# Gate tiles of a recurrence and a convolution moved beside attention heads, and kept in DRAM until they are used

## The chip, the cores and the metric

The kernel runs on one core of a Trainium2 chip. The metric is the device time of one execution in microseconds (us); lower is better. The core has a matrix engine (PE, with its weight loads as PEld), a vector engine (DVE), an activation engine (ACT), a general engine (POOL) and a queue for transfers (SP). Each takes its instructions strictly in its own order; engines wait for one another by semaphores.

## The reference

Two networks of two layers each run one after the other on 512 tokens of 1024 features in fp32. Only the second matters here. Each of its layers projects the normed input and mixes three branches, each with a gate:

```
h = rms_norm(x, norm_g[l]);  proj = h @ w_in[l]
y_nsa  = nsa_attention(...)            # 8 heads of 64: two softmax attentions and a compressed one
y_lru  = rg_lru(u_lru, ...)            # 4-tap conv, two block-diagonal gates, scan along time
y_conv = conformer_conv(ga, gb, ...)   # u = ga*sigmoid(gb); 31-tap conv; layer norm; silu; @ w_pw2
mixed  = concat(y_nsa * silu(z_nsa), y_lru * silu(z_lru), y_conv * silu(z_conv))
x = x + mixed @ w_out[l]
```

`z_nsa`, `z_lru` and `z_conv` are columns of `proj` (512 each), so they depend only on `h`.

## The kernel before

Each product is made of three matmuls of high and low halves (`mm3`, L213 to L215; "split" means that ACT writes the high half, L204 or L237, and DVE or POOL the rest, L206, L208, L238). `w_tiles` makes 128 output columns by 512 tokens at a time: 24 matmuls with 512 moving columns over K = 1024, called a dense tile here. Weights come in slabs of 512 KB through SP; for the gate columns the low halves were computed earlier and are loaded too (`stored`, L273).

The heads (`nsa`) work in halves of 256 tokens: scores (L382), softmax over DVE, ACT and POOL (L389 to L394), transposes (L417, L425), values (L432), the compressed part (L1357), and at the end of a half `av_out` (L439 on ACT, L440 on DVE). A half is a long chain of small matmuls with waits.

The order in which the program issues work is that of the Python code, which a scheduler at build time then merges: it interleaves the heads with whatever dense tiles are ready and stand near. `PLACES` says how many pieces of side work (`work`: four parts of the convolution with their 31 taps, L1412; `part(0)` and `part(2)` of the recurrence, which end in a square root, L1522, and scans, L1526; its two gates, L1530) are issued after each stage of `mix2`: here four after heads 0, 4, 1, 5, one after heads 2, 6, 3, 7, and the rest behind the second `gated`. Last comes `conv_out`: for each of four token blocks b0 to b3 a transpose (L1442), statistics (L1444, L1446), a reciprocal root in two small POOL instructions (L364, L365) and the normed block (L1448); then for each of four column tiles transposes (L1453), two activations (L1455, L1456), a product (L1457) and a split; then the four z_conv tiles (`z`, L1466), and at last the product with `w_pw2` (`pw`, 48 matmuls) and `w_out` (`out2`, 288 matmuls; its output adds to the residual y, which is loaded from DRAM into the four buffers of tag `ac`).

The words "H" and "the norm chain" below stand for the end of the last matmul of the last head (the last L1357) and for the way from there through `conv_out` to the first `pw` matmul.

Of the kernel before, what the change touches and what calls it, by code (L numbers as in the profile page):

```python
# [69 lines left out]
class Net:  # L70
# [15 lines left out]
    def name(self, s):  # L86
# [2 lines left out]

    BUFS = {  # L90
        1: dict(raw=4, xt=2, ph=2, ac=4, pt=4, s=9, tmp=2, tiny=10, tm=12, rs=4, os=2, wh=4, wl=4, qk=13, q4=3, q3=1, sig=3, m8=3, sc=3, lraw=2, llo=2),
        2: dict(raw=2, xt=2, ph=2, ac=4, pt=6, s=7, os=2, wh=4, wl=4, qk=12, q4=4, sig=3, zt=2, cg=4, nt=2, gt=2, cu=2, cv=3, lr=2, lw=2, tiny=10, tm=12, rs=4),
    }
    FIRST = {F32: dict(ac=(1024, 4), sc1=(256, 1), sc2=(384, 1), sc3=(512, 1), iw=(32, 1), lf=(24, 2)), F32R: dict(dv=(512, 1), row=(512, 1))}
    SECOND = {F32: dict(cu=(512, 2), cs=(512, 2), ct=(2048, 1), par=(192, 2), sp=(4, 2), gates=(96, 1), pos=(16, 2), tmp=(256, 2)), F32R: dict(vc=(512, 2), kc=(128, 1))}
# [8 lines left out]
    ORDER = 'ISFDftdxBbzy'  # L104
    VIA = "q"
    LOP2 = "01"
    PLACES = [0, 0, 0, 0, 0, 4, 1, 8]
    PBUFS = dict(mm=3, ss=2, tr=2, av=1, acc=1)

    def phase(self, block, kept):  # L110

        self.block = block
        self.hold = self.last_load.ins if block > 1 and self.last_load else None
        self.places = {}
        for dtype, tags in kept.items():
            at = self.kept[dtype]
            for tag, (words, n) in tags.items():
                self.places[tag] = [at + i * words for i in range(n)]
                at += n * words
            assert at <= self.KEPT[dtype]  # L120

    def t(self, tag, shape, dtype=F32):
        if tag in self.places:
# [1307 lines left out]

        return c, [lambda j=j: part(j) for j in range(4)]

    def conv_out(self, l, h, c, par):

        nc, a = self.nc, self.a
        norm = self.t("nt", [P, 4, T])
        for b in range(NT):
            tok = slice(b * P, (b + 1) * P)
            tr = self.ps("tr")  # L1440
            for j in range(4):
                nc.tensor.transpose(tr[:, j * P:(j + 1) * P], c[j][:, tok], self.ident)  # L1442
            st = self.small([P, 6])
            nc.vector.bn_stats(st, tr)  # L1444
            mv = self.small([P, 2])
            nc.vector.bn_aggr(mv, st)  # L1446
            r = self.rstd(mv[:, 1:2], 1e-6)
            nc.vector.tensor_scalar(norm[:, b], tr, mv[:, 0:1], r, op0=OP.subtract, op1=OP.mult)  # L1448
        act = []
        for j in range(4):  # L1450
            tr = self.ps("tr")
            for b in range(NT):
                nc.tensor.transpose(tr[:, b * P:(b + 1) * P], norm[:, b, j * P:(j + 1) * P], self.ident)  # L1453
            s, v = self.t("sig", [P, T]), self.t("cg", [P, T])
            nc.scalar.activation(v, tr, AF.Identity, scale=par["g"][:, j:j + 1], bias=par["b"][:, j:j + 1])  # L1455
            nc.scalar.activation(s, tr, AF.Tanh, scale=par["hg"][:, j:j + 1], bias=par["hb"][:, j:j + 1])  # L1456
            nc.vector.scalar_tensor_tensor(s, s, 1.0, v, op0=OP.add, op1=OP.mult)  # L1457
            t = self.t("qk", [P, 2, T], F32R)
            self.split(s, t[:, 0], t[:, 1], scale=0.5)
            act.append(t)  # L1460
        zs = self.t("nt", [P, 4, T])
        sz = [zs[:, j] for j in range(4)]

        def z(j, ps):
            s = sz[j]
            nc.scalar.activation(s, ps, AF.Tanh, scale=0.5)  # L1466
            nc.vector.scalar_tensor_tensor(s, s, 1.0, ps, op0=OP.add, op1=OP.mult)

        self.w_tiles(a["w_in"][l], [[(3864 + j * P, P)] for j in range(4)], h, z, lows=self.lows[l])
        out = []  # L1470

        def pw(j, ps):
            s = sz[j]
            nc.vector.tensor_mul(s, s, ps)
            out.append(self.mixed(s))

        self.hold = self.last_load.ins
        self.w_tiles(a["conv_w_pw2"][l], [[(j * P, P)] for j in range(4)], (_Stack(act, 0), _Stack(act, 1)), pw, K=4)
        return out

    def lru(self, l, h, par):

        nc, a = self.nc, self.a
        g, out = {}, {}
        blocks = self.t("pt", [P, 2, 4, P])
        nc.gpsimd.memset(blocks, 0.0)
        for i, name in enumerate(("lru_w_a", "lru_w_i")):
            src = a[name][l].rearrange("(j r) i o -> r i j o", r=2)
# [29 lines left out]
        def part(j0):  # L1518
            da, db = [self.t("lw", [P, 2, T]) for _ in range(2)]
            self.w_tiles(a["w_in"][l], [[(1816 + j * P, P)] for j in (j0, j0 + 1)], h,  # L1520
                         lambda j, ps: emit(j0 + j, ps, da[:, j], db[:, j]), lows=self.lows[l])
            nc.scalar.activation(db, db, AF.Sqrt)  # L1522
            for i in range(2):
                v = g[j0 + i]
                nc.vector.scalar_tensor_tensor(db[:, i], v, 0.5, db[:, i], op0=OP.mult, op1=OP.mult)
                nc.vector.tensor_tensor_scan(v, da[:, i], db[:, i], 0.0, OP.mult, OP.add)  # L1526

        def z(j, ps):
            s = self.gate_silu(ps)
            nc.gpsimd.tensor_mul(g[j], s, g[j])  # L1530
            out[j] = g[j]

        def gate(j0):
            self.w_tiles(a["w_in"][l], [[(2328 + j * P, P)] for j in (j0, j0 + 1)], h, lambda j, ps: z(j0 + j, ps),
                         lows=self.lows[l])

        return out, [lambda: part(0), lambda: part(2), lambda: gate(0), lambda: gate(2)]

    def mix2(self, l, h, tables):
        nc, a = self.nc, self.a  # L1540
        par = self.params2(l)
# [147 lines left out]
```

## Time and profile before

| | us |
|---|---|
| median of 3 runs (lowest, highest) | 2550.74 (2550.54, 2554.34) |
| the profiled execution's own time | 2551.98 |
| its span | 2550.2 |
| PE busy | 2472.7 (97%) |
| DVE, ACT, POOL busy | 1630.3, 1231.7, 729.7 |
| second network, layer 0: last head matmul, first `pw` matmul, last `w_out` matmul start | 2024, 2065.60, 2142 |
| layer 1: first `pw` matmul | 2465.78 |

PE's busy time counts each matmul from its start to its modelled end, and matmuls overlap; how closely they follow one another tells more. Where nothing waits, one with 512 columns starts every 0.23 us.

### The profile page before, as it was taken

To read this page: it belongs to the slowest core of one execution; us is meant where nothing else is said; L and a number is where in the kernel's file an instruction comes from. 1 tells how busy PE (TensorE), PEld (TensorE's weight loads), DVE (VectorE), ACT (ScalarE), POOL (GpSimd) and SP (SyncE) were. 2 spreads that over 40 slices of the span, in tenths; PEclk is the share of its full clock that TensorE was granted. 3 is DMA by queue.
4 is the path that set the end of the run, shared out by engine and by line. 5 is a ranking of instruction groups with operands and counts; after the bars stand their busy time and mean duration, and the time that the engine had idled before them with its cause. 6 is when DMAs were issued, how large, how long until landed. Compare 5 with 4: busy or idle time off the path is not lost.

```text
span 2550.2 us, 35074 instructions
## 1 busy us (share of the span) xinstructions
PE 2472.7 (97%) x12660; PEld 2097.7 (82%) x12660; DVE 1630.3 (64%) x3126; ACT 1231.7 (48%) x2271; POOL 729.7 (29%) x845
## 2 busy tenths in 40 slices
PE   8989999999999998999999999998999899999998
PEld 8878888888888887888888888887988688988777
DVE  4985865654344669659465544346699755589874
ACT  5665643344333255665323343233575742576760
POOL 5621560122110264206002122004353312353320
PEclk9999999999999999999999999999999999999999
DMA  5203225366543332132435656334444143554151
GB/s 167 83 16 85 74 83 187 123 197 224 170 161 94 96 85 66 46 86 82 133 119 169 203 190 222 93 97 121 140 143 130 43 150 114 149 153 127 51 178 40
DMA packets 276654, 312.00 MB, mean 122 GB/s; under 512 B 25792, under 2 KB 221696, under 8 KB 276480
## 3 DMA queue, kind: packets, MB, share of 16 engines
q1 hardware_dynamic: 276480, 309.76, 39.4%
q8 instruction: 100, 1.64, 0.3%
q14 instruction: 74, 0.61, 0.1%
HBM read 274.84 MB, written 34.87 MB: 121 GB/s over the span
## 4 chain that ended last, share of the span: by engine, by line
PE 82%; DVE 9%; ACT 3%; DMA 2%; issue 2%; POOL 1%; SPq 0%; DVEq 0%; ACTq 0%; POOLq 0%
PE mm L214 19%; PE mm L215 18%; PE mm L213 18%; PE ss L382 3%; PE av L432 3%; PE ss L214 3%; PE ss L215 3%; PE ss L213 3%; PE tr L417 2%; PE av L215 1%; PE av L214 1%; PE av L213 1%; PE tr L215 1%; PE tr L214 1%; PE tr L213 1%
## 5 line engine op out<-in xcount | busy, mean ns | idle before, releaser
L238 DVE TENSOR_TENSOR wl<-raw,wh 128x1024 fp32r<-128x1024 f32 (+3 forms) x308 | 392.8, 1279 | 326.9 <-ACT wh L237 317.9
L237 ACT ACTIVATE wh<-raw 128x1024 fp32r<-128x1024 f32 (+6 forms) x358 | 361.3, 1013 | 448.8 <-PE tr L215 176.9
L213 PE MATMUL mm<-xt,wh 128*128 128x512 f32 x1456 | 574.4, 394 | 2.1 <-DVE sig L1376 2.1
L215 PE MATMUL mm<-xt,wl 128*128 128x512 f32 x1456 | 572.2, 393 | 2.8 <-DVE wl L238 2.8
L214 PE MATMUL mm<-xt,wh 128*128 128x512 f32 x1456 | 573.8, 394 | 0.0
L215 PEld LDWEIGHTS mm<-xt,wl 128*128 128x128 f32 x1456 | 275.0, 189 | 59.0 <-DVE wl L238 4.4
L213 PEld LDWEIGHTS mm<-xt,wh 128*128 128x128 f32 x1456 | 275.1, 189 | 57.3 <-DVE sig L1376 2.5
L214 PEld LDWEIGHTS mm<-xt,wh 128*128 128x128 f32 x1456 | 274.9, 189 | 54.5 <-issue 0.5
L260 POOL TENSOR_TENSOR llo<-lraw,llo 128x1024 fp32r<-128x1024 f32 x48 | 116.3, 2435 | 378.3 <-ACT llo L259 363.4
L213 PE MATMUL mm<-wh,xt 128*128 128x256 f32 (+6 forms) x624 | 190.4, 311 | 10.1 <-ACT wh L237 8.8
L215 PE MATMUL mm<-wh,xt 128*128 128x256 f32 (+6 forms) x624 | 191.9, 310 | 5.8 <-DVE xt L206 5.7
L214 PE MATMUL mm<-wl,xt 128*128 128x256 f32 (+6 forms) x624 | 192.6, 311 | 2.4 <-DVE wl L238 1.6
L364 POOL TENSOR_SCALAR tiny<-tiny 128x1 f32<-128x1 f32 x24 | 11.9, 495 | 516.7 <-DVE tiny L863 477.7
L391 ACT ACTIVATE s<-s,tm 128x128 f32<-128x128 f32 (+1 forms) x216 | 120.5, 558 | 64.4 <-DVE tm L389 57.2
L214 PE MATMUL mm<-wl,qk 128*128 128x512 f32 x352 | 136.2, 390 | 0.0
L215 PE MATMUL mm<-wh,qk 128*128 128x512 f32 x352 | 136.0, 389 | 0.0
L213 PE MATMUL mm<-wh,qk 128*128 128x512 f32 x352 | 134.7, 389 | 0.0
L394 POOL TENSOR_SCALAR s<-s,tm,kept 128x128 f32<-128x128 f32 (+3 forms) x128 | 78.4, 612 | 195.0 <-DVE tm L393 174.0
L213 PEld LDWEIGHTS mm<-wh,xt 128*128 128x128 f32 x624 | 119.6, 194 | 12.8 <-ACT wh L237 9.2
L215 PEld LDWEIGHTS mm<-wh,xt 128*128 128x128 f32 x624 | 120.4, 193 | 8.3 <-DVE xt L206 7.2
L214 PEld LDWEIGHTS mm<-wl,xt 128*128 128x128 f32 x624 | 120.7, 194 | 5.4 <-DVE wl L238 2.5
L1412 DVE SCALAR_TENSOR_TENSOR acc<-kept,acc 128x511 f32<-128x511 f32 (+6 forms) x168 | 124.1, 739 | 1.6
(373 smaller groups left out, 5256.8 us busy)
## 6 DMA issues: line engine op xcount, KB each, us to landing
raw<-in_w_in SPq DMA_DIRECT2D x84, 512.0 KB, 4.2
raw<-in_w_ff_in SPq DMA_DIRECT2D x64, 512.0 KB, 4.0
raw<-in_w_ff_out SPq DMA_DIRECT2D x64, 512.0 KB, 3.8
raw<-in_w_in SPq DMA_DIRECT2D x104, 256.0 KB, 3.8
low<-llo SPq DMA_DIRECT2D x48, 512.0 KB, 2.8
wl<-low SPq DMA_DIRECT2D x48, 512.0 KB, 3.7
raw<-in_w_out SPq DMA_DIRECT2D x40, 512.0 KB, 3.8
lraw<-in_w_in SPq DMA_DIRECT2D x48, 256.0 KB, 6.1
```

Of the source, the lines that this page charges most:

```text
L213: mm(out, A[0], B[0], start=start, stop=False)
L214: mm(out, A[0], B[1], start=False, stop=False)
L215: mm(out, A[1], B[0], start=False, stop=stop)
L237: self.nc.scalar.activation(hi, raw, AF.Copy)
L238: (self.nc.gpsimd if self.lo_on_pool else self.nc.vector).tensor_sub(lo, raw, hi.bitcast(F32))
L260: nc.gpsimd.tensor_sub(lo, raw, lo.bitcast(F32))
L382: self.nc.tensor.matmul(s, u[:, tok], v[:, :n], start=i == 0, stop=i == len(k) - 1)
L391: nc.scalar.activation(p, p, AF.Exp, bias=m, scale=-1.0, accum_out=den)
L394: nc.gpsimd.tensor_scalar(p, p, r, 1.0 if gate is None else gate, op0=OP.mult, op1=OP.mult)
L417: nc.tensor.transpose(tr[:, kb * P:(kb + 1) * P], p[:, kb * P:(kb + 1) * P], self.ident)
L432: nc.tensor.matmul(av[:, 256 - m.shape[-1]:], v[:, kb], m, start=start and kb + i == 0, stop=stop and kb == n - 1 and i == 1)
L1412: nc.vector.scalar_tensor_tensor(acc[0][:, d:], u[:, :T - d], w[:, k], acc[0][:, d:], op0=OP.mult, op1=OP.add)
```

## The change

- `PLACES` becomes strings of piece names. After heads 0, 4, 1, 5: the four convolution parts and `part(0)` of the recurrence (`abcdp`). After heads 2, 6, 3, 7: the four z_conv tiles and the four z_lru tiles (`zgh`). Behind the second `gated`: `part(2)`, then `gated(0)` and `gated(2)` (`qmn`).
- A gate tile is finished as before (`gate_silu`) but goes to DRAM (`side_gates`: 8 writes of 256 KB a layer). It is read back later (`back`): z_conv as one read of 1 MB into `nt`, z_lru as two reads of 512 KB into the `lw` buffers, which hold `part(2)`'s coefficients before that. POOL then multiplies (L1546 of the changed kernel).
- The tag `ac` is gone; the residual's four buffers lie on the kept space of the convolution's input, side sums and result.

PE, DVE, ACT and POOL have as many instructions as before (12646, 3032, 2049, 850); SP has 22 more (774 to 796).

```diff
-        2: dict(raw=2, xt=2, ph=2, ac=4, pt=6, s=7, os=2, wh=4, wl=4, qk=12, q4=4, sig=3, zt=2, cg=4, nt=2, gt=2, cu=2, cv=3, lr=2, lw=2, tiny=10, tm=12, rs=4),
+        2: dict(raw=2, xt=2, ph=2, pt=6, s=7, os=2, wh=4, wl=4, qk=12, q4=4, sig=3, zt=2, cg=4, nt=2, gt=2, cu=2, cv=3, lr=2, lw=2, tiny=10, tm=12, rs=4),
-    PLACES = [0, 0, 0, 0, 0, 4, 1, 8]
+    PLACES = ["", "", "", "", "", "abcdp", "zgh", "qmn"]
+        if "cu" in self.places:
+            self.places["ac"] = [self.places["cu"][0] + i * 1024 for i in range(4)]
+    def side_gates(self, l, h, c0, js, dst):
+
+        def z(i, ps):
+            s = self.gate_silu(ps)
+            self.nc.sync.dma_start(dst[:, js[i]], s)
+
+        self.w_tiles(self.a["w_in"][l], [[(c0 + j * P, P)] for j in js], h, z, lows=self.lows[l])
+
+    def back(self, src, t):
+
+        with self.tc.issue_after(self.last_load.ins):
+            self.nc.sync.dma_start(t, src)
+        return t
+
...
-        zs = self.t("nt", [P, 4, T])
+        out = []
+        zs = self.back(zd, self.t("nt", [P, 4, T]))
         sz = [zs[:, j] for j in range(4)]
-
-        def z(j, ps):
-            s = sz[j]
-            nc.scalar.activation(s, ps, AF.Tanh, scale=0.5)
-            nc.vector.scalar_tensor_tensor(s, s, 1.0, ps, op0=OP.add, op1=OP.mult)
-
-        self.w_tiles(a["w_in"][l], [[(3864 + j * P, P)] for j in range(4)], h, z, lows=self.lows[l])
-        out = []
...
-        def z(j, ps):
-            s = self.gate_silu(ps)
-            nc.gpsimd.tensor_mul(g[j], s, g[j])
-            out[j] = g[j]
+        zd = self.dram([P, 4, T])
...
+        def gated(j0):
+            z = self.back(zd[:, j0:j0 + 2], self.t("lw", [P, 2, T]))
+            for i in range(2):
+                j = j0 + i
+                nc.gpsimd.tensor_mul(g[j], z[:, i], g[j])
+                out[j] = g[j]
...
+        zd = self.dram([P, 4, T])
+        work = dict(zip("pqghmn", lru), z=lambda: self.side_gates(l, h, 3864, (0, 1, 2, 3), zd))
+        work.update((k, lambda f=f: (f(), self.run(steps, len(steps)))) for k, f in zip("abcd", glu))
+
+        def more(place):
+            for k in self.PLACES[place]:
+                work[k]()
```

What this does to the order of the engines is seen at three places of layer 0 of the second network.

On PE, in the norm chain of the kernel before, the transposes of column tiles (L1453, tr from nt) stand among the matmuls of the z_conv tiles (mm from xt, the normed input):

```order
L215 MATMUL mm_18977<-xt_12749,wl_18947 128x512
L213 MATMUL mm_18977<-xt_12749,wh_18946 128x512
L214 MATMUL mm_18977<-xt_12750,wh_18946 128x512
L1453 MATMUL tr_18911<-kept_66,nt_18832 128x128 x4
L215 MATMUL mm_18977<-xt_12749,wl_18947 128x512
L213 MATMUL mm_18977<-xt_12749,wh_18946 128x512
L1453 MATMUL tr_18924<-kept_66,nt_18832 128x128 x4
L214 MATMUL mm_18977<-xt_12750,wh_18946 128x512
L215 MATMUL mm_18977<-xt_12749,wl_18947 128x512
L213 MATMUL mm_18977<-xt_12749,wh_18946 128x512
```

In the changed kernel, at the same place (L1458 and L1469 are its transposes, mm from qk is `pw`), only matmuls of `w_out` (av, ss from wh and wl) are left ahead, and none between:

```order
L217 MATMUL av_19186<-wh_19222,qk_18967 128x512
L217 MATMUL ss_19187<-wh_19222,qk_18967 128x512
L217 MATMUL ss_19188<-wh_19222,qk_18967 128x512
L1458 MATMUL tr_19022<-kept_66 128x128 x4
L1469 MATMUL tr_19035<-kept_66,nt_18982 128x128 x4
L1469 MATMUL tr_19048<-kept_66,nt_18982 128x128 x4
L1469 MATMUL tr_19061<-kept_66,nt_18982 128x128 x4
L1469 MATMUL tr_19074<-kept_66,nt_18982 128x128 x4
L215 MATMUL mm_19095<-qk_19045,wh_19091 128x512
L215 MATMUL mm_19112<-qk_19045,wh_19091 128x512
L215 MATMUL mm_19135<-qk_19045,wh_19131 128x512
L216 MATMUL mm_19095<-qk_19045,wh_19091 128x512
```

The dense tiles have gone ahead of the last heads: of the 144 dense matmuls of gate tiles that lay between H and `pw`, none is left there; 18 of `w_out` are.

On POOL, at the end of a layer's heads, before: the roots of b0 to b3 (tiny) and the multiplies of the recurrence's gates (gt):

```order
L364 TENSOR_SCALAR tiny_18842<-tiny_18840 128x1
L365 TENSOR_TENSOR tiny_18842<-tiny_18842,kept_66 128x1
L364 TENSOR_SCALAR tiny_18855<-tiny_18853 128x1
L365 TENSOR_TENSOR tiny_18855<-tiny_18855,kept_66 128x1
L364 TENSOR_SCALAR tiny_18868<-tiny_18866 128x1
L365 TENSOR_TENSOR tiny_18868<-tiny_18868,kept_66 128x1
L1530 TENSOR_TENSOR gt_18436<-sig_18705,gt_18436 128x512
L1530 TENSOR_TENSOR gt_18436<-sig_18734,gt_18436 128x512
L364 TENSOR_SCALAR tiny_18881<-tiny_18879 128x1
L365 TENSOR_TENSOR tiny_18881<-tiny_18881,kept_66 128x1
L1530 TENSOR_TENSOR gt_18613<-sig_18775,gt_18613 128x512
L1530 TENSOR_TENSOR gt_18613<-sig_18804,gt_18613 128x512
```

The same in the changed kernel (L366 and L367 the root, L1546 the multiplies, lw the tile read back, "x2" two in a row):

```order
L366 TENSOR_SCALAR tiny_18992<-tiny_18990 128x1
L367 TENSOR_TENSOR tiny_18992<-tiny_18992,kept_66 128x1
L366 TENSOR_SCALAR tiny_19005<-tiny_19003 128x1
L367 TENSOR_TENSOR tiny_19005<-tiny_19005,kept_66 128x1
L366 TENSOR_SCALAR tiny_19018<-tiny_19016 128x1
L367 TENSOR_TENSOR tiny_19018<-tiny_19018,kept_66 128x1
L1546 TENSOR_TENSOR gt_17710<-lw_18950,gt_17710 128x512 x2
L1546 TENSOR_TENSOR gt_18895<-lw_18954,gt_18895 128x512 x2
L366 TENSOR_SCALAR tiny_19031<-tiny_19029 128x1
L367 TENSOR_TENSOR tiny_19031<-tiny_19031,kept_66 128x1
```

All four multiplies now stand ahead of the root of b3.

On DVE, changed kernel, the same place (L1462 statistics, L1464 the normed block, L210 splits; qk from gt is the recurrence's output):

```order
L1464 TENSOR_SCALAR nt_18982<-tr_18996,tiny_19003,tiny_19005 128x512
L1462 BN_AGGR tiny_19016<-tiny_19014 128x2
L1464 TENSOR_SCALAR nt_18982<-tr_19009,tiny_19016,tiny_19018 128x512
L1460 BN_STATS tiny_19027<-tr_19022 128x6
L1462 BN_AGGR tiny_19029<-tiny_19027 128x2
L210 SCALAR_TENSOR_TENSOR qk_18970<-gt_17710,qk_18970 128x512
L210 SCALAR_TENSOR_TENSOR qk_18973<-gt_17710,qk_18973 128x512
L210 SCALAR_TENSOR_TENSOR qk_18976<-gt_18895,qk_18976 128x512
L210 SCALAR_TENSOR_TENSOR qk_18979<-gt_18895,qk_18979 128x512
L1464 TENSOR_SCALAR nt_18982<-tr_19022,tiny_19029,tiny_19031 128x512
L1473 SCALAR_TENSOR_TENSOR sig_19040<-sig_19040,cg_19041 128x512
```

The four splits of the recurrence's output, which wait for POOL's multiplies, stand ahead of the normed block b3. Before, one of the four stood ahead of it and three behind.

## Rows read from the trace of the kernel before

**Rows 1.** The page: the chain that ended last, by engine.

```profile
PE 82%; DVE 9%; ACT 3%; DMA 2%; issue 2%; POOL 1%; SPq 0%; DVEq 0%; ACTq 0%; POOLq 0%
```

**Rows 2.** Layer 0: length, busy us (instructions) PE, PEld, DVE, ACT, POOL; clock, DMA.

```profile
1914.00:1960.00 46.00, 46.00 (x255) 39.71 (x254) 42.80 (x101) 27.59 (x62) 15.11 (x21) 1.00 0.45 129
1960.00:2010.00 50.00, 44.73 (x274) 36.45 (x272) 40.91 (x132) 32.27 (x89) 17.31 (x29) 0.99 0.12 40
2010.00:2040.00 30.00, 28.17 (x128) 20.56 (x128) 25.59 (x45) 26.71 (x43) 7.85 (x11) 0.96 0.27 89
2066.00:2142.40 76.40, 76.40 (x341) 63.19 (x341) 32.50 (x45) 16.65 (x19) 4.46 (x7) 1.00 0.35 107
```

**Rows 3.** Dense matmuls of 1914 to 1960, then 1960 to 2010, L215's third.

```profile
L215 PE MATMUL mm<-xt,wl 128*128 128x512 f32 x47 | 18.5, 394 | 0.0
...
L215 PE MATMUL mm<-xt,wl 128*128 128x512 f32 x11 | 4.3, 391 | 0.0
```

**Rows 4.** Layer 1's stretches that answer to layer 0's second and third.

```profile
2360.00:2410.00 50.00, 44.64 (x274) 35.81 (x274) 40.78 (x132) 34.05 (x94) 17.77 (x30) 1.00 0.11 36
2410.00:2440.00 30.00, 27.35 (x119) 20.00 (x119) 25.79 (x43) 26.20 (x41) 7.61 (x11) 0.94 0.24 73
```

**Rows 5.** PE's timeline around two gaps: start, length, instruction, idle time before.

```profile
2036.35 0.50 PE L213 MATMUL mm<-xt,wh 128*128 128x512 f32 x1 [1.83 <-DVE sig L1376]
2036.69 0.40 PE L214 MATMUL mm<-xt,wh 128*128 128x512 f32 x1
...
2434.74 0.33 PE L1453 MATMUL tr<-kept,nt 128*128 128x128 f32 x1 [1.87 <-DVE nt L1448]
...
2435.72 0.63 PE L214 MATMUL mm<-xt,wh 128*128 128x512 f32 x1
...
2438.28 0.63 PE L214 MATMUL mm<-xt,wh 128*128 128x512 f32 x1
```

**Rows 6.** DVE's half ends among the heads alone, 1970 to 2010.

```profile
L440 DVE TENSOR_TENSOR os<-av,kept 64x256 f32<-64x256 f32 x6 | 2.5, 416 | 0.4 <-ACT kept L439 0.2
```

**Rows 7.** Timeline: last head matmul, half end, normed b3, first pw matmul.

```profile
2023.78 0.45 PE L1357 MATMUL av<-qk,kept 128*128 128x256 f32 x2
...
2027.47 0.42 DVE L440 TENSOR_TENSOR os<-av,kept 64x256 f32<-64x256 f32 x1
...
2041.63 0.80 DVE L1448 TENSOR_SCALAR nt<-tr,tiny,tiny 128x512 f32<-128x512 f32 x1
...
2065.60 0.39 PE L213 MATMUL mm<-qk,wh 128*128 128x512 f32 x1
```

**Rows 8.** Instructions of the norm chain, 2010 to 2066, by line and form.

```profile
L1530 POOL TENSOR_TENSOR gt<-sig,gt 128x512 f32<-128x512 f32 x4 | 6.3, 1577 | 5.0 <-DVE gt L1526 4.7 <-DVE sig L1376 0.3
L1526 DVE TENSOR_TENSOR_SCAN gt<-lw,lw 128x512 f32<-128x512 f32 x4 | 4.7, 1210 | 0.0
L1456 ACT ACTIVATE sig<-tr,kept 128x512 f32<-128x512 f32 x4 | 3.2, 795 | 0.0
L208 DVE SCALAR_TENSOR_TENSOR qk<-gt,qk 128x512 fp32r<-128x512 f32 x4 | 3.1, 786 | 1.2 <-ACT qk L204 1.2
L1444 DVE BATCH_NORM_STATS2 tiny<-tr 128x6 f32<-128x512 f32 x4 | 2.8, 695 | 0.4 <-PE tr L1442 0.4
L365 POOL TENSOR_TENSOR tiny<-tiny,kept 128x1 f32<-128x1 f32 x4 | 2.6, 647 | 0.3
L1448 DVE TENSOR_SCALAR nt<-tr,tiny,tiny 128x512 f32<-128x512 f32 x4 | 3.2, 803 | 1.2 <-POOL tiny L365 1.2
L204 ACT ACTIVATE qk<-gt 128x512 fp32r<-128x512 f32 x4 | 2.5, 632 | 2.0 <-POOL gt L1530 1.9
L364 POOL TENSOR_SCALAR tiny<-tiny 128x1 f32<-128x1 f32 x4 | 1.7, 425 | 19.9 <-DVE tiny L1446 19.8
L1375 ACT ACT_TABLE_LOAD x1 | 1.3, 1283 | 0.0
```

**Rows 9.** DMA issues, 1900 to 2150: KB each, median us to landing.

```profile
wl<-low SPq DMA_DIRECT2D x12, 512.0 KB, 3.6
```

More of the change, by code (lines that the diff above doesn't have):

```diff
@@ L1432, in conv_glu, with conv_out @@
         return c, [lambda j=j: part(j) for j in range(4)]
-    def conv_out(self, l, h, c, par):
+    def side_gates(self, l, h, c0, js, dst):
[7 more added lines that the diff above has]
+        return t
+    def conv_out(self, l, c, par, zd):
         nc, a = self.nc, self.a
@@ L1526, in part @@
                 nc.vector.tensor_tensor_scan(v, da[:, i], db[:, i], 0.0, OP.mult, OP.add)
-        def z(j, ps):
-            s = self.gate_silu(ps)
-            nc.gpsimd.tensor_mul(g[j], s, g[j])
-            out[j] = g[j]
+        zd = self.dram([P, 4, T])
         def gate(j0):
-            self.w_tiles(a["w_in"][l], [[(2328 + j * P, P)] for j in (j0, j0 + 1)], h, lambda j, ps: z(j0 + j, ps),
-                         lows=self.lows[l])
-        return out, [lambda: part(0), lambda: part(2), lambda: gate(0), lambda: gate(2)]
+            self.side_gates(l, h, 2328, (j0, j0 + 1), zd)
+        def gated(j0):
[4 more added lines that the diff above has]
+                out[j] = g[j]
+        return out, [lambda: part(0), lambda: part(2), lambda: gate(0), lambda: gate(2), lambda: gated(0), lambda: gated(2)]
     def mix2(self, l, h, tables):
@@ L1544, in mix2 @@
         y, lru = self.lru(l, h, par)
-        work = [lambda f=f: (f(), self.run(steps, len(steps))) for f in glu] + lru
-        more = lambda place: self.run(work, self.PLACES[place])
+        zd = self.dram([P, 4, T])
[4 more added lines that the diff above has]
+                work[k]()
         proj = self.nsa_project(l, h, tables, more)
@@ L1572, in mix2 @@
         first = [self.mixed(x[j]) for x in (nsa, y) for j in range(4)]
-        return first + self.conv_out(l, h, c, par)
+        return first + self.conv_out(l, c, par, zd)
     def mixed(self, s):
```

## The prediction

> **What bounds the kernel now.** The chain that ended last is PE for 82% of the span [rows 1], so a change is worth what it does to the time in which PE waits or runs its matmuls further apart than it could. PE's busy share does not show that: its matmuls overlap, and a stretch can read as nearly full while they start late. So I read the stretches around the change [rows 2], and in each I count the matmuls and price them by the pace at which they follow one another where nothing waits. A dense one takes 0.2275 us (341 matmuls, 336 of them dense, fill 76.4 us, [rows 2]). In 1914 to 1960, where dense tiles and heads are mixed, 255 records stand in 46 us, 140 of them dense (47 for each of two lines, 46 for the third, [rows 3]); these take 31.9 us, which leaves 14.1 us for 115 small ones, 0.12 us each. That is just their pace when they run back to back (0.11 for 128 columns, 0.12 for 256, 0.18 for 384), so **a mixed stretch loses nothing**. In 1960 to 2010 there are 274 records with only 32 dense (11, 11, 10, [rows 3]): 7.3 us, and 242 small ones at 0.126 make 30.5, so 37.8 of 50 us are work and **12.2 us are lost**. This is where the heads run alone, from 1970 on. From 2010 to 2040 the same count gives 3.3 us lost: one gap of 1.83 us before a z tile [rows 5] and a granted clock of 0.96 over 30 us (1.2 us) [rows 2]. After 2040 nothing is lost. Layer 0 thus loses about 16 us. Layer 1, counted the same way, loses 12.5 us in 2360 to 2410 and 5.5 in 2410 to 2440, together 18, with a clock of 0.94 and a gap of 1.87 [rows 4, 5].
>
> The change removes no matmul and adds none. What it is worth is the losses after, less these 16 and 18.
>
> **The heads.** The z_conv and z_lru tiles and `part(0)` go beside the heads. By the order of the changed kernel the dense tiles last until about two and a half halves before the end; only 78 head matmuls or so stand without them. Alone, the heads lost 11.9 us over 40 us with 6 half ends [rows 2, 6], 2 us a half. So 2.5 halves lose 5 us. Where they are mixed the loss is zero now; but DVE was busy for 42.8 of 46 us there [rows 2], 93%. `part(0)` brings 11.9 us of DVE work (two tiles with four taps, two products, a scan each) beside 10.9 us of its own dense matmuls, which makes 54.7 of 56.9 us, 96%. Still below PE, but the heads wait for DVE at many places: I add 1 us (bounds 0 and 5, the latter if all that DVE gets in addition beyond its present share comes late). Sum for the heads **6 us**, bounds 2 (one half alone, DVE hidden) and 12 (no better than now).
>
> When does this end? The orders differ first at about 1913 us. From there to H the changed order holds 356 dense matmuls (81.0 us), 24 and 22 score matmuls of 512 and 384 columns (9.4), 154 of 256 (18.2), 196 of 128 (22.0) and eight block-diagonal ones of the recurrence (6.9): 137 us. With 6 lost, H is at about 2056, against 2024 before [rows 7]; 32 us later, because 144 dense matmuls have gone ahead of it.
>
> **The norm chain.** Before, those 144 dense matmuls, 32.8 us, lay between H and `pw` and covered the chain from the last head to the activated tiles; `pw` started 41.4 us after H [rows 7]. After, PE has between H and `pw` 28 transposes and 18 `w_out` matmuls, 7.2 us. So the chain becomes visible. I walk it from H, with durations of [rows 8] unless said otherwise.
> 1. The last half end on DVE came 3.7 us after the last head matmul before [rows 7]; the same instructions surround it after. PE's next `w_out` matmuls reuse its bank, so they start at H+3.7, and the transposes of b2 behind them end at 6.4.
> 2. DVE then has a scan (1.2), statistics of b1 (0.7), b0 normed (0.8), the gate product (0.7), b1's mean (0.2), statistics of b2 (0.7), the split of the last nsa tile (0.7), b1 normed (0.8): 9.5 and b2's mean 9.7. POOL's root of b2 (0.43 and 0.65) ends at 10.8.
> 3. POOL has the four multiplies next, 1.577 each: 17.1. They wait for nothing else, as far as I see: the read-backs use the buffers of `part(2)`, free after its last scan at about H+5, and 512 KB land 3.6 us after issue [rows 9].
> 4. Behind the multiplies stands b3's root (1.1: 18.2), and on DVE the four splits of the recurrence's output (0.63 on ACT and 0.79 after the last multiply: 18.5) and then b3 normed: 19.4.
> 5. Transposes (0.3), the first activation (0.8), an activation table (1.3), the second (0.8), the next tile's two, which stand ahead of the first split (1.3), the split (0.6): `pw` starts at **H+24.5**.
>
> Of these PE works 7.2 and waits **17.3 us**. Bounds: with multiplies as short as a scan (1.2) and the half end 2 us earlier, 14; from above, the kernel before had b3 normed 18.2 us after H [rows 7] with two multiplies ahead of its root where there are now four, which gives 21.4 in place of 19.4, and a read-back that takes twice the 3.6 us [rows 9], behind the 1 MB of z_conv, adds 1: 20.
>
> **The clock.** After its gap of 1.87 us layer 1's matmuls started 0.43 us apart (seven in 2.56 us, of which the first and the last stand in [rows 5]), at a granted clock of a half, 1.2 GHz, in place of 0.23; after the gap of 1.83 in layer 0 they went on at the full 2.4 GHz [rows 5]. With the one ahead of them that is eight dense matmuls at 0.2 us more each, 1.6. A wait of some 10 us on end is longer than both; I take **1.6 us** a layer, bounds 0 and 3.2. The Trainium skill (TensorE: Matmul & The Clock Gate, "Loop structure matters more than you think") says that a matmul after a long wait runs cold, and that products should follow one another without such waits; it speaks against this change. One of the two gaps of this trace agrees with it, the other does not; by the page alone the term is certain, by the rows it may be absent, and the forecast would be 3 us lower.
>
> **Others.** The residual's last four loads now wait for the transposes of the convolution's result (H+10) and are wanted when the first `w_out` tile is finished, after `pw`: later than H+28. Even at three times the 3.6 us of a load of 512 KB [rows 9] they are covered; without that cover they would cost PE those 11 us. The write-backs of 256 KB and two more waits on SP lie among weight loads of the mixed stretch, of which PE waited for none. Behind the reads on SP stand those residual loads and the `w_out` slabs after the first four; the slabs are wanted after `pw`, too. From `pw` on, 302 dense matmuls are left, as fast as now.
>
> **Sum.** Layer 0: 6 + 17.3 + 1.6 = 24.9 lost after, 16 before: +8.9. Layer 1: 24.9 against 18: +6.9. Together **+15.8 us**: 2567.8 for the profiled execution's 2551.98, or on the median, 1.2 below it, **2566.5**.
>
> **Rivals.**
> - *No change* (2546 to 2556). Heads filled better and the chain short: 2 + 14 + 1 = 17 a layer, as now. For it: the mixed stretch loses nothing today. Against it: PE must wait behind POOL's 6.3 us in every case.
> - *Faster*, about 2541. It takes losses below 13 a layer, 3 to 5 under those of today. The mechanism is the last halves: if the dense tiles reach to the end of the heads (loss 0) and the statistics of the blocks run while the last half is still under way, so that the roots of b0 to b2 are past when the half ends, the multiplies start at H+6 and `pw` at H+19.5: 12 lost. It decides from a `pw` start of some H+19. Against it: the transposes of b2 and b3 stand behind `w_out` matmuls that wait for the half end.
> - *DVE the bound* of the mixed stretch: the heads lose 12 as before, 31 a layer, +28: 2579. For it: 96%.
> - *The read-back late*: landing at H+16 in place of 9, behind 1 MB and the residual, moves the multiplies by 5: +26, 2576. Against it: the transfers have room (a DMA share of 0.12 in 1960 to 2010, [rows 2]).
>
> **How the numbers follow.** The forecast has a chance of 0.55 (2556 to 2575), no change 0.15, faster 0.11, DVE 0.13, read-back 0.06. Within 0.2% (5.1 us, about what a measurement here can tell from no change) thus lies 0.15, below it 0.11, above 0.74. The range leaves a tenth at either end: 2547 to 2582.
>
> **What would show it.** Right: H near 2056 and `pw` near 2081 in layer 0, PE with waits of 15 to 20 us between, ended by DVE's normed b3 and ACT's activations; POOL's four multiplies in one piece ahead of b3's root; PE's loss in 1970 to 2010 near zero. Wrong: `pw` within 20 us of H, or H past 2062, or PE waiting for transfers.

## The result, and the profile after

| | before | after |
|---|---|---|
| median in one comparison, us (runs) | 2552.4 (4) | 2567.32 (4) |
| lowest, highest | 2550.54, 2554.34 | 2565.39, 2569.01 |
| ratio of the times, 95% interval | | 1.0055, 1.0043 to 1.0067 |
| profiled execution, its span | 2551.98, 2550.2 | 2565.39, 2563.6 |

The changed kernel is 14.9 us (0.55%) slower. The forecast was 2566.5, 15.8 above the 2550.74 of the kernel before that it started from.

The page of the changed kernel gives the chain that ended last, by engine, and the answer to [rows 1]:

```profile
PE 82%; DVE 9%; ACT 3%; issue 2%; DMA 2%; POOL 1%; SPq 0%; DVEq 0%; POOLq 0%; ACTq 0%
```

PE's share is what it was; on this level nothing can be seen. The stretches show more. These are the windows of the changed kernel, with the columns of [rows 2]; the last line is layer 1's norm chain:

```profile
1914.00:1960.00 46.00, 46.00 (x251) 38.88 (x249) 44.07 (x99) 27.82 (x61) 18.62 (x22) 1.00 0.41 137
1960.00:2010.00 50.00, 49.37 (x262) 41.36 (x261) 34.50 (x89) 33.75 (x69) 9.47 (x15) 1.00 0.59 188
2010.00:2040.00 30.00, 29.53 (x175) 25.59 (x174) 19.15 (x57) 19.03 (x44) 11.81 (x13) 1.00 0.19 58
2040.00:2060.00 20.00, 17.23 (x96) 12.72 (x96) 16.59 (x38) 17.04 (x33) 3.86 (x6) 1.00 0.20 58
2060.00:2090.00 30.00, 18.04 (x67) 14.10 (x68) 20.50 (x31) 13.82 (x20) 9.89 (x12) 0.72 0.31 105
2090.00:2152.00 62.00, 62.00 (x277) 51.39 (x276) 29.86 (x43) 13.90 (x16) 3.48 (x6) 1.00 0.34 115
...
2463.00:2493.00 30.00, 17.86 (x67) 14.11 (x68) 20.55 (x30) 13.86 (x20) 9.89 (x12) 0.72 0.32 111
```

Before, PE's poor stretch was 1960 to 2010, where the heads ran alone [rows 2]. Now that stretch is full (49.37 of 50 us, and transfers of 188 GB/s in place of 40), and the poor one is 2060 to 2090: PE is busy for 18.04 of 30 us, at a granted clock of 0.72. It lies behind the heads, and layer 1 has its like.

Now the norm chain, in the timeline of the changed kernel (PE, DVE, POOL, ACT and SP's queue, put together in order of time; answers to [rows 7]):

```profile
2058.26 0.46 PE L1359 MATMUL av<-qk,kept 128*128 128x256 f32 x2
2061.48 0.42 DVE L442 TENSOR_TENSOR os<-av,kept 64x256 f32<-64x256 f32 x1
2061.96 0.51 PE L215 MATMUL av<-wh,qk 128*128 128x512 f32 x1 [2.80 <-DVE os L442]
2062.31 0.89 SPq L1447 DMA_DIRECT2D lw<-spill  x2
2062.69 0.63 PE L217 MATMUL av<-wh,qk 128*128 128x512 f32 x1
...
2065.25 0.62 PE L217 MATMUL av<-wh,qk 128*128 128x512 f32 x1
...
2068.88 0.55 POOL L367 TENSOR_TENSOR tiny<-tiny,kept 128x1 f32<-128x1 f32 x1
2069.39 5.82 POOL L1546 TENSOR_TENSOR gt<-lw,gt 128x512 f32<-128x512 f32 x4
2070.33 0.33 PE L1469 MATMUL tr<-kept,nt 128*128 128x128 f32 x1 [1.01 <-DVE nt L1464]
2071.35 5.28 DVE L210 SCALAR_TENSOR_TENSOR qk<-gt,qk 128x512 fp32r<-128x512 f32 x4 [0.26 <-ACT qk L206]
2075.90 0.55 POOL L367 TENSOR_TENSOR tiny<-tiny,kept 128x1 f32<-128x1 f32 x1
2076.55 0.80 DVE L1464 TENSOR_SCALAR nt<-tr,tiny,tiny 128x512 f32<-128x512 f32 x1
2077.41 3.04 PE L1469 MATMUL tr<-kept,nt 128*128 128x128 f32 x13 [6.75 <-DVE nt L1464]
2078.70 1.28 ACT L1472 ACT_TABLE_LOAD   x1
2082.68 1.65 PE L215 MATMUL mm<-qk,wh 128*128 128x512 f32 x3 [2.24 <-ACT qk L206]
2084.13 0.63 PE L216 MATMUL mm<-qk,wh 128*128 128x512 f32 x1
2084.56 0.63 PE L217 MATMUL mm<-qk,wl 128*128 128x512 f32 x1
```

H is 2058.72 (2058.26 and 0.46). PE then waits four times: 2.80 for the last half end, 1.01 and 6.75 for normed blocks, 2.24 for the first activated tile, 12.8 us together. POOL's four multiplies start 1.3 us ahead of the longest wait and run on through it in one piece; b3's root follows them, and on DVE the four splits stand in the same stretch. `pw` starts at 2082.68, H+24.0. Twice the dense matmuls run 0.43 us apart: from 2062.69 to 2065.25 six steps take 2.56, and from 2084.13 to 2084.56 one takes 0.43. The 13 transposes from 2077.41 on follow one another at 0.21 (3.04 us for all), about twice the 0.11 that the prediction prices for one of 128 columns.

The DMA issues of the changed kernel from 1900 to 2150 (KB each, median us to landing), for the transfers that are new:

```profile
nt<-spill SPq DMA_DIRECT2D x1, 1024.0 KB, 4.8
lw<-spill SPq DMA_DIRECT2D x2, 512.0 KB, 4.6
```

Counted and priced as in the prediction, from the first to the last head matmul ("heads") and from H to 5 us past the start of `pw` ("end"), PE loses this, layer 0 / layer 1 in us:

| | heads | end | of it waits | and half clock | `pw` after H | layer's length |
|---|---|---|---|---|---|---|
| before | 14.0 / 13.1 | 2.0 / 4.8 | 1.8 / 2.6 | 0 / 1.6 | 41.4 / 44.1 | 262.8 / 264.2 |
| after | 6.0 / 6.1 | 18.5 / 18.1 | 12.8 / 12.7 | 2.9 / 2.6 | 24.0 / 23.8 | 271.3 / 270.5 |

(The length is that from the first matmul of the heads' compressed part to the last of `w_out`; "half clock" is the number of matmuls that stand 0.43 apart by 0.2 us, so it leaves the slow transposes out.) The losses grow by 8.5 and 6.3, and the layers by 8.5 and 6.3: inside these stretches the account is closed. Outside them the two executions differ too. The changed kernel comes to layer 0 2.2 us later, and its way from the last `w_out` matmul of layer 0 to the first of the heads' compressed part in layer 1 takes 131.9 us in place of 135.5, at a granted clock of 0.99 in place of 0.96. So the spans differ by 13.4 us, not by 14.8.

### The profile page after: what moved, and what is told of

It reads as the page before. It is cut to its first block, busy times and chain, and to the rows that moved or that the text cites. A ratio compares the mean times of both kernels' runs of the same rounds, so it can differ in the third digit from the quotient of the medians.

```text
span 2563.6 us, 35115 instructions
## 1 busy us (share of the span) xinstructions
PE 2468.6 (96%) x12660; PEld 2098.8 (82%) x12660; DVE 1631.8 (64%) x3126; ACT 1233.7 (48%) x2271; POOL 734.0 (29%) x845
## 4 chain that ended last, share of the span: by engine, by line
PE 82%; DVE 9%; ACT 3%; issue 2%; DMA 2%; POOL 1%; SPq 0%; DVEq 0%; POOLq 0%; ACTq 0%
PE mm L216 19%; PE mm L215 19%; PE mm L217 19%; PE ss L384 3%; PE ss L217 3%; PE ss L216 3%; PE ss L215 3%; PE av L434 3%; PE tr L419 2%; PE av L215 1%; PE av L216 1%; PE av L217 1%; PE tr L217 1%; PE tr L216 1%; PE tr L215 1%
## 5 line engine op out<-in xcount | busy, mean ns | idle before, releaser
L240 DVE TENSOR_TENSOR wl<-raw,wh 128x1024 fp32r<-128x1024 f32 (+3 forms) x308 | 393.2, 1280 | 303.3 <-ACT wh L239 288.2
L215 PE MATMUL mm<-xt,wh 128*128 128x512 f32 x1456 | 573.0, 394 | 0.2
L215 PEld LDWEIGHTS mm<-xt,wh 128*128 128x128 f32 x1456 | 274.6, 189 | 54.2 <-DVE sig L1378 0.6
L215 PE MATMUL mm<-wh,xt 128*128 128x256 f32 (+6 forms) x624 | 189.9, 311 | 10.1 <-ACT wh L239 8.9
L366 POOL TENSOR_SCALAR tiny<-tiny 128x1 f32<-128x1 f32 x24 | 12.6, 526 | 505.2 <-DVE tiny L865 476.5
L215 PE MATMUL mm<-wh,qk 128*128 128x512 f32 x352 | 134.8, 389 | 0.0
L215 PEld LDWEIGHTS mm<-wh,xt 128*128 128x128 f32 x624 | 119.1, 193 | 12.8 <-ACT wh L239 9.3
L391 DVE CUSTOM_DVE_ANT_0 s<-ss,kept 128x128 f32<-128x128 f32 (+1 forms) x216 | 103.5, 479 | 37.4 <-PE ss L384 35.5
```

Of the source, the lines that this page charges most:

```text
L215: mm(out, A[0], B[0], start=start, stop=False)
L240: (self.nc.gpsimd if self.lo_on_pool else self.nc.vector).tensor_sub(lo, raw, hi.bitcast(F32))
L391: nc.vector.tensor_tensor_reduce(p, s, bias, -0.125, 3e38, OP.add, OP.min, m)
```

## The experiments

Times are medians (lowest to highest, runs), ratios those to the kernel before in the same comparison, whose median was 2552.1 to 2553.5 in all of them. Diffs are against the changed kernel, unless said otherwise. The table behind the last experiment has the losses of each.

**The convolution's gate made in the chain again.** Of the three moves (z_conv, z_lru, `part(0)`) the first is undone, and its read-back with it.

```diff
-    PLACES = ["", "", "", "", "", "abcdp", "zgh", "qmn"]
+    PLACES = ["", "", "", "", "", "abcdp", "gh", "qmn"]
...
-        zs = self.back(zd, self.t("nt", [P, 4, T]))
+        zs = self.t("nt", [P, 4, T])
...
+        self.w_tiles(a["w_in"][l], [[(3864 + j * P, P)] for j in range(4)], h, z, lows=self.lows[l])
```

> The z_conv tiles are made in conv_out again and never go to DRAM; z_lru stays beside the heads. Theory (the norm chain is bare after the last head): 24 dense matmuls of z_conv and 48 of w_out then lie between the last head and pw, 16.4 us of cover where there were 4.1. The wait between the last head and pw falls from 15 to some 4 us a layer, one of the two clock drops goes (1.6): about 2541 (2536 to 2550). Rival (the traffic to DRAM and on SP costs the 15 us): half of the traffic is left, so half of the loss: about 2559. Rival (z_conv is needed to fill the heads): the heads lose 8 a layer again, 2556.

Measured 2557.07 (2549.9 to 2559.43, 10 runs), ratio 1.0011 (1.0002 to 1.0021): 10 us below the changed kernel, 16 above what I expected. By its trace the end loses 10.6 and 10.8 in place of 18.5 and 18.1. Between the last head and `pw` now lie 72 dense matmuls, 24 of z_conv and 48 of `w_out`, where the changed kernel has 18; they do cover, but not all of it. PE's timeline, the waits of over 1 us in layer 0's chain:

```profile
2057.08 0.50 PE L215 MATMUL mm<-xt,wh 128*128 128x512 f32 x1 [1.80 <-DVE nt L1484]
2065.47 0.50 PE L216 MATMUL av<-wl,qk 128*128 128x512 f32 x1 [1.52 <-DVE wl L240]
2074.87 1.20 PE L1469 MATMUL tr<-kept,nt 128*128 128x128 f32 x9 [1.26 <-DVE nt L1464]
2078.07 1.12 PE L1469 MATMUL tr<-kept,nt 128*128 128x128 f32 x4 [2.00 <-ACT sig L1472]
```

Work that fills a wait also brings work for DVE (its own gate products L1484, weight splits L240), and the chain gets longer: b3 is normed at H+20.4 and `pw` starts at H+29.9. The median alone lay near the times that both rivals gave. The trace decides against them: the heads lose 1.5 us a layer more than in the changed kernel, not the 7 or so that the second rival needs, and the gain is in the chain, where no wait of PE is for a transfer.

**The multiplies written behind the normed blocks**, to take POOL's four multiplies and DVE's four splits out of b3's way.

```diff
-    PLACES = ["", "", "", "", "", "abcdp", "zgh", "qmn"]
+    PLACES = ["", "", "", "", "", "abcdp", "zgh", "q"]
...
-        first = [self.mixed(x[j]) for x in (nsa, y) for j in range(4)]
-        return first + self.conv_out(l, c, par, zd)
+        first = [self.mixed(nsa[j]) for j in range(4)]
+        act = self.conv_act(c, par)
+        work["m"]()
+        work["n"]()
+        first += [self.mixed(y[j]) for j in range(4)]
+        return first + self.conv_pw(l, act, zd)
```

> The recurrence's multiplies and splits are written behind the convolution's normed blocks. Theory (they stand in the norm chain): b3 is normed 4.4 us earlier a layer, since its root waits for nothing but its own statistics, and pw starts as much earlier: 2558 (2555 to 2561). Rival (the chain is held by something else, the last half or ACT): no change, 2567.

Measured 2568.06 (2560.24 to 2569.69, 4 runs), ratio 1.0063 (1.0046 to 1.0080): as the changed kernel, and 10 above what I expected. The timeline of POOL and DVE shows that the edit did only half of what it says (L1551 are the multiplies here):

```profile
2067.13 4.93 POOL L1551 TENSOR_TENSOR gt<-lw,gt 128x512 f32<-128x512 f32 x4
2073.00 0.81 DVE L1464 TENSOR_SCALAR nt<-tr,tiny,tiny 128x512 f32<-128x512 f32 x1 [4.17 <-POOL tiny L367]
```

The scheduler put the splits behind b3 and left the multiplies ahead of its root. DVE, which had the splits to do there, now waits 4.17 us. b3 comes 1.2 us earlier (H+17.4), where the multiplies alone take 4.9. So this run says little of the multiplies. Its profiled execution (2560.24) also lies below the three others (2567.56 to 2569.69), so its losses in the table aren't those of its median.

**The read-backs in buffers of their own**, in place of `part(2)`'s.

```diff
-        2: dict(raw=2, xt=2, ph=2, pt=6, s=7, os=2, wh=4, wl=4, qk=12, q4=4, sig=3, zt=2, cg=4, nt=2, gt=2, cu=2, cv=3, lr=2, lw=2, tiny=10, tm=12, rs=4),
+        2: dict(raw=2, xt=2, ph=2, pt=6, s=7, os=2, wh=4, wl=4, qk=12, q4=4, sig=3, zt=2, cg=4, nt=2, gt=2, cu=2, cv=3, lr=2, lw=2, lz=2, tiny=10, tm=12, rs=4),
...
-            z = self.back(zd[:, j0:j0 + 2], self.t("lw", [P, 2, T]))
+            z = self.back(zd[:, j0:j0 + 2], self.t("lz", [P, 2, T]))
```

> The two read-backs of z_lru get buffers of their own, so that they need not wait for the recurrence's coefficients to be used up. Theory (POOL comes to the multiplies only after b2's root, when the tiles have landed): no change, 2564 to 2570. Rival (the read-back is late): the multiplies start with b2's root or earlier, 5 us a layer, 2557.

Measured 2561.68 (2559.36 to 2564.6, 6 runs), ratio 1.0034 (1.0022 to 1.0046): 5.6 us below the changed kernel. My "no change" fell, and the rival's 2557 was not reached either. Its timeline, POOL and DVE:

```profile
1996.02 2.54 POOL L1546 TENSOR_TENSOR gt<-lz,gt 128x512 f32<-128x512 f32 x2 [5.54 <-DMA lz<-spill]
...
2062.67 3.42 POOL L1546 TENSOR_TENSOR gt<-lz,gt 128x512 f32<-128x512 f32 x2
...
2074.02 0.81 DVE L1464 TENSOR_SCALAR nt<-tr,tiny,tiny 128x512 f32<-128x512 f32 x1 [1.02 <-POOL tiny L367]
```

Two of the four multiplies are done 60 us before H, beside the heads. The other two follow b0's root. b3 is normed at H+15.3 (18.6 with the shared buffers), `pw` starts at H+20.6 (24.0), and the end loses 15.2 in both layers.

**The residual's place alone**, the other part of the change, put on the kernel before:

```diff
-        2: dict(raw=2, xt=2, ph=2, ac=4, pt=6, s=7, os=2, wh=4, wl=4, qk=12, q4=4, sig=3, zt=2, cg=4, nt=2, gt=2, cu=2, cv=3, lr=2, lw=2, tiny=10, tm=12, rs=4),
+        2: dict(raw=2, xt=2, ph=2, pt=6, s=7, os=2, wh=4, wl=4, qk=12, q4=4, sig=3, zt=2, cg=4, nt=2, gt=2, cu=2, cv=3, lr=2, lw=2, tiny=10, tm=12, rs=4),
...
+        if "cu" in self.places:
+            self.places["ac"] = [self.places["cu"][0] + i * 1024 for i in range(4)]
```

> The kernel before with one part of the change alone: the residual's four buffers lie on the convolution's kept space. Theory: its loads are covered by pw and w_out; no change, 2549 to 2555. Rival (half of the residual comes late, behind the transposes of the convolution's result): 5 us a layer, 2562.

Measured 2552.06 (2549.1 to 2556.89, 10 runs), ratio 0.9997 (0.9988 to 1.0006). It costs nothing, as expected.

**The normed blocks between the last heads.** All of the change stays; `conv_norm` (statistics, roots and normed blocks) is written between the second and the third of the last four heads, and the normed blocks take the place of the convolution's result.

```diff
-            for n in ns:
+            for i, n in enumerate(ns):
+                if i == 2 and between:
+                    between()
...
-        norm = self.t("nt", [P, 4, T])
+        norm = c["t"]
...
-        o = heads([2, 6, 3, 7])
+        norm = []
+        o = heads([2, 6, 3, 7], lambda: norm.append(self.conv_norm(c)))
```

> The convolution's transposes and normed blocks are written between the second and the third of the last four heads, and the normed blocks take the convolution result's own place; the rest is the changed kernel. In PE's order the normed blocks are then ahead of the last two and a half halves, and 50 w_out matmuls lie between the last head and pw. Theory (the bare norm chain costs 15 us of waits and 3 of half clock a layer): both go but for some 2 us, the heads lose 7 as in the changed kernel: 16 a layer less than it, 2567 - 32 = 2535 (2528 to 2545). Rival (the gates' way through DRAM, or DVE in the mixed stretch, is what costs): 2560 or more. Rival (the heads now wait for the norm chain): the loss moves there, 2555.

Measured 2550.91 (2549.0 to 2557.0, 11 runs), ratio 0.9999 (0.9990 to 1.0008): 16 us below the changed kernel, as fast as before, and 16 above what I expected. The end loses 3.8 and 5.0 only, and `pw` starts at H+19.3. But the heads lose 9.3 and 14.5. Layer 1 shows how, in its windows and PE's timeline:

```profile
2420.00:2430.00 10.00, 7.32 (x40) 6.02 (x38) 10.00 (x25) 5.19 (x10) 4.37 (x6) 1.00 0.21 61
2430.00:2440.00 10.00, 7.14 (x33) 5.61 (x33) 7.12 (x23) 3.89 (x14) 5.20 (x9) 0.66 0.11 44
...
2432.65 1.19 PE L384 MATMUL ss<-q,q 128*128 128x128 f32 x4 [5.33 <-DVE tm L395]
```

DVE is busy for all of the 10 us (normed blocks, the recurrence's taps, weight splits), and the heads' softmax stands behind them in its queue; behind PE's wait the granted clock falls to 0.66 over the next 10 us. This is what the rival with the heads waiting for the norm chain said (2555). All writes to DRAM and all read-backs are still there, and its two layers together take 1.2 us less than before (525.8 and 527.0): traffic is not what the change costs.

**The whole chain ahead of the last head** (the same call at `i == 3`, the activations with it), and the same **with the read-backs' own buffers**.

```diff
-            for n in ns:
+            for i, n in enumerate(ns):
+                if i == 3 and between:
+                    between()
...
-        o = heads([2, 6, 3, 7])
+        act = []
+        o = heads([2, 6, 3, 7], lambda: act.extend(self.conv_act(c, par)))
```

> The whole of the convolution's norm, transposes, activations and splits are written ahead of the last of the four heads. In PE's order some three halves then run alone ahead of the gate tiles, 147 dense matmuls of gate tiles come after the last head, and nothing is bare. Theory: the end costs nothing, the heads lose 9 to 11: 13 to 15 a layer less than the changed kernel, 2540 (2533 to 2550). Rival (filling the heads is what counts, as little can be lost at the end): no better than the kernel before, 2552.

> As the one with the whole norm chain ahead of the last head, and with buffers of their own for the two read-backs of z_lru. Theory (the multiplies cost something only where the norm chain behind them is bare): the same time as without, within 3 us. Rival (the read-back costs in any case): 5 us faster.

Measured 2597.65 (2593.73 to 2599.3, 4 runs), ratio 1.0177 (1.0162 to 1.0191), and 2595.76 (2592.45 to 2598.67, 4 runs), ratio 1.0171 (1.0156 to 1.0186). The first missed by 58. The end loses nothing now, but the heads lose 38.8 and 38.7. Two windows of the first:

```profile
1960.00:2030.00 70.00, 49.27 (x271) 38.02 (x269) 54.49 (x162) 47.59 (x115) 23.36 (x40) 0.87 0.00 1
2040.00:2110.00 70.00, 70.00 (x314) 56.94 (x313) 32.38 (x43) 29.78 (x40) 5.14 (x3) 1.00 0.66 214
```

For 70 us next to nothing arrives from DRAM (DMA share 0.00): no dense tile lies there, and heads and chain wait for each other on PE, at a granted clock of 0.87. The rival's 2552 was missed as well. The dense tiles come behind, at full pace, with nothing left to cover. That the own buffers change nothing here is as expected: the multiplies cost time only where the chain is bare.

**The normed blocks between the heads, with z_conv's tiles written earlier** (the edit of the normed blocks between the last heads, and one place more):

```diff
-    PLACES = ["", "", "", "", "", "abcdp", "zgh", "qmn"]
+    PLACES = ["", "", "", "", "", "abcdpz", "gh", "qmn"]
```

> As the one with the normed blocks between the last heads, but the z_conv tiles are written ahead of the last four heads, so that in PE's order b0 to b3 are normed some 30 matmuls later, nearer to the last half. Theory: nothing is bare at the end and DVE has fewer norms while it is busiest; the loss is that of the heads, 7 a layer, and 4 at the end: 2545 (2538 to 2552). Rival (the norms cost the heads the same wherever they stand): 2551, as with the z_conv tiles later.

Measured 2561.14 (2556.17 to 2562.8, 12 runs), ratio 1.0026 (1.0017 to 1.0036): a miss of 16, and of 10 for the rival. The end loses 1.7 and 0.6, the heads 16.9 and 23.2. In the waits of layer 0, 2020 to 2070 (us in total, times, longest), the scores wait on PE for the softmax, as in the case before:

```profile
PE ss L384 <- DVE tm L391: 3.4, 1, 3.4
```

That wait is only a part of the heads' loss. Another is the clock: over the same 50 us the granted one is 0.92, which is 4 us of full speed.

**Combinations**, to see whether the parts add up: late splits with own buffers; z_conv in the chain with own buffers; all three. Their diffs are those above put together; the lines that tell them apart are, in this order:

```diff
+    PLACES = ["", "", "", "", "", "abcdp", "zgh", "q"]
+            z = self.back(zd[:, j0:j0 + 2], self.t("lz", [P, 2, T]))
...
+    PLACES = ["", "", "", "", "", "abcdp", "gh", "qmn"]
+            z = self.back(zd[:, j0:j0 + 2], self.t("lz", [P, 2, T]))
...
+    PLACES = ["", "", "", "", "", "abcdp", "gh", "q"]
+            z = self.back(zd[:, j0:j0 + 2], self.t("lz", [P, 2, T]))
```

> Read-backs in buffers of their own, and the recurrence's splits written behind the convolution's normed blocks, so that neither multiplies nor splits stand ahead of b3's root. Theory (what is left of the chain is the last half's end and the roots): b3 normed at 14 us after the last head and pw at 19.5, 1 us a layer better than with the read-backs alone: 2560 (2556 to 2563). Rival (the splits cost as much as the multiplies): 2555.

> z_conv made in conv_out again, and the read-backs of z_lru in buffers of their own. Theory (each of the two takes a part of the bare chain, cover 6 us and the multiplies 3 us a layer, and they add up): 2552 (2548 to 2556). Rival (with cover on PE the multiplies cost nothing more): 2557.

> Three edits of the changed kernel together: z_conv made in conv_out again (24 of its dense matmuls and 48 of w_out then lie between the last head and pw), the read-backs of z_lru in buffers of their own, and the recurrence's splits written behind the normed blocks. Theory (each shortens or covers the bare chain, the heads stay filled): the heads lose 7.5 a layer, the end 5, against 16 and 18 in the kernel before: 2546 (2541 to 2551), faster than both. Rival (the splits are not in the way once PE has cover): 2555, as without that edit.

Measured 2560.57 (2558.58 to 2562.17, 9 runs), ratio 1.0026 (1.0016 to 1.0036): as expected, with b3 at H+14.0. Then 2554.78 (2552.62 to 2559.72, 12 runs), ratio 1.0007 (0.9998 to 1.0016): some 3 above. Last 2550.04 (2546.4 to 2556.26, 12 runs), ratio 0.9990 (0.9980 to 0.9999): 4 above what I expected, 17 us below the changed kernel, and 0.1% below the kernel before, which is less than a measurement can tell here; its layers are about as long as those before (263.9 and 263.6). They are also as long, together, as those without the late splits (527.5 and 527.2): in the profiled executions these two kernels differ by 4.6 us, but the one with all three comes to the heads of layer 0 6.9 us earlier. So the traces do not put the difference between their medians down to the splits. Step by step, these edits give back what the change cost, and no more that these runs can tell.

| losses, us (layer 0 / 1) | heads | end |
|---|---|---|
| z_conv in the chain | 7.5 / 7.5 | 10.6 / 10.8 |
| late splits | 6.0 / 6.4 | 15.9 / 16.4 |
| own buffers | 6.2 / 6.7 | 15.2 / 15.2 |
| late splits, own buffers | 6.2 / 6.6 | 14.6 / 14.2 |
| z_conv in the chain, own buffers | 7.4 / 8.2 | 8.4 / 10.2 |
| all three | 7.4 / 7.4 | 9.7 / 10.0 |
| normed blocks between heads | 9.3 / 14.5 | 3.8 / 5.0 |
| the same, z_conv earlier | 16.9 / 23.2 | 1.7 / 0.6 |
| whole chain ahead of the last head | 38.8 / 38.7 | -0.2 / -0.2 |

Added up over both layers, less the 33.9 of the kernel before, these losses give the time that each ratio stands for to within some 3 us (the late splits alone set aside).

## Why the prediction was right

The result and its mechanism came as forecast: what the heads gain, the chain behind them loses twice over. How the chain's loss divides between waits and clock did not.

- **The heads.** Forecast 6 us lost, measured 6.0 and 6.1. From 1970 to 2010, where 11.9 were lost before, 0.3 are. "DVE the bound" fell: in 1914 to 1960 DVE is busy for 44.07 of 46 us, the 96% forecast, and the stretch loses 0.1.
- **When they end.** H came at 2058.7, not 2056. That is no loss near the heads: the compressed part's matmuls that start at 1906.42 in the trace before start at 1908.65 after, 2.2 us later, ahead of the first place where the orders differ. Executions differ by so much there: in the trace of the kernel with the residual's place alone the same point, and all since 1420, is 2.4 us late as well, and in that with the late splits it is not (1906.34). The priced sum itself holds; its "eight block-diagonal ones" are 16 in the trace, 0.43 us apart, which make the same 6.9.
- **The norm chain.** `pw` at H+24.0 and 23.8 (24.5 forecast), b3 normed at H+18.6 and 18.4 (19.4). The terms err little: the half end comes 0.5 us early (H+3.2), the steps from it to the multiplies take 0.4 longer (they start at H+10.7, as forecast), the multiplies 0.5 less (5.82 for 6.3), and from b3 to `pw` it is 5.4 (5.1).
- **Waits and clock.** Here the division was wrong. PE's waits were to be 17.3 us, and a sign of being right was "waits of 15 to 20 us"; they are 12.8 and 12.7. The clock was to take 1.6 us, at most 3.2; it takes 2.9 and 2.6 from the dense matmuls, and 13 transposes at 0.1 more each make 1.4 beside that, some 4 us in all. The step took one drop in a layer, behind the waits. There are two, one behind the wait of 2.80 and one that begins within that of 6.75 and outlasts the start of `pw`. The Trainium skill (TensorE: Matmul & The Clock Gate, "Loop structure matters more than you think") says that matmuls after a long wait run cold. The 13 transposes behind the wait of 6.75 agree with it. Most of this slow work lies ahead of `pw`, inside the time that the chain takes: up to `pw` 24.0 less 7.2 of work is 16.8 (16.6 in layer 1), where 17.3 was forecast, and behind it 1.6 and 1.4 are lost, where the clock's 1.6 was. So the chain's length was forecast well, and the waits came out short because PE worked slowly in part of them. What the slow work ahead of `pw` costs in time is not shown, as PE waits behind it in any case. The sum is 18.5 and 18.1 against 18.9.
- **The sum.** 24.5 and 24.2 lost (24.9 forecast), 16.0 and 17.9 before (16 and 18): +14.8 for +15.8. The medians differ by 14.9; that this agrees to 0.1 is luck, as the profiled executions differ by 13.4.
- **What was incomplete.** "They wait for nothing else, as far as I see", of the multiplies, holds in the order as built: the read-backs, issued at 2062.31 (H+3.6), land some 4.6 us later, before POOL comes to them. But the place itself hangs on their buffers. With buffers of their own two multiplies leave the chain and 5.6 us come back. The rival "read-back late" was thus wrong as put, a read-back that lands behind its multiply; its place was set earlier, where the order was made.
- **The faster rival** named `pw` at H+19 as its turning point, and the normed blocks between the heads reach it (19.3). The time that it gave, 2541, still did not come (2550.91), since the blocks' work on DVE then delays the heads.
- **Others.** The residual costs nothing (0.9997). Traffic costs nothing that shows: with the normed blocks between the heads a kernel with all of it runs in the time before.

The runs show that the chain's bareness is the cause, from two sides: dense tiles put back into it return 10 us, and its normed blocks taken out return 16. How the 12.8 us of waits divide into multiplies, splits and roots is shown only for the two multiplies that own buffers release; late splits beside own buffers take another 1.1 us off the median, which is within the noise. With all four behind b3's root it was not tried: in the one run written for it the scheduler left them ahead.

## What to carry to other kernels

Dense work beside a chain of short dependent steps is a cover, and moving it to another chain uncovers the first: before the move, walk the chain that loses it and price it bare. A buffer shared with an earlier step fixes more than the time of a transfer; it also fixes where the work that reads it can stand in an engine's queue. And work taken out of one chain into a place where DVE is full comes back as waits of whoever stands behind it there.

## What had not been expected of the hardware

The same waits don't always bring the half clock. PE's timeline with all three edits, layer 0, two waits at the end of the chain:

```profile
2072.25 0.66 PE L1469 MATMUL tr<-kept,nt 128*128 128x128 f32 x4 [2.00 <-ACT sig L1472]
2073.59 0.80 PE L215 MATMUL tr<-wh,qk 128*128 128x512 f32 x1 [0.68 <-ACT sig L1472]
2074.18 0.63 PE L216 MATMUL tr<-wl,qk 128*128 128x512 f32 x1
2074.61 0.63 PE L217 MATMUL tr<-wh,qk 128*128 128x512 f32 x1
```

And with z_conv in the chain and own buffers, layer 0, the same instructions after the same two waits (the waits ahead of these are 1.79 and 1.51 us with all three edits, and 1.80, 1.49 and 1.03 in this kernel):

```profile
2080.68 0.66 PE L1469 MATMUL tr<-kept,nt 128*128 128x128 f32 x4 [2.00 <-ACT sig L1472]
2082.02 0.50 PE L215 MATMUL tr<-wh,qk 128*128 128x512 f32 x1 [0.68 <-ACT sig L1472]
2082.36 0.39 PE L216 MATMUL tr<-wl,qk 128*128 128x512 f32 x1
2082.59 0.40 PE L217 MATMUL tr<-wh,qk 128*128 128x512 f32 x1
```

The first runs 0.43 us apart (granted clock 0.50 from 2074 to 2076, which is 1.2 GHz), the second 0.23 apart (1.00 from 2082 to 2086, 2.4 GHz). In layer 1 of the second kernel the same waits, within 0.04 us, are followed by seven steps of 0.43. What decides it stays open; it is worth 2.6 us in a layer.

POOL's multiply of 128x512 takes very different times. With the late splits, where DVE mostly waits, each of the eight takes 1.26 to 1.27 us. In the changed kernel two take 1.26, and the two that run beside DVE's splits 1.70 and 1.71. With own buffers they take from 1.27 to 2.19, the longest beside statistics and scans, and with z_conv in the chain as well up to 2.56. It is one instruction, with a spread of a factor of two that seems to go with what DVE does at the time. No run isolates it.
